# Encoder block: the Fourier channel transform multiplied into the weights, the softmax division moved to a^T

## The chip, the core and the metric

The kernel runs on one core of a Trainium2 chip. TensorE (PE) multiplies matrices into PSUM banks of 512 fp32 columns; its weight loads (PEld) run beside its matmuls. VectorE (DVE), ScalarE (ACT) and GpSimd (POOL) work element by element, and SyncE (SP) mostly issues DMAs. Each engine runs its own instructions strictly in order and waits on semaphores of the others. The metric is the device time of one execution in microseconds (us), the median of several runs. Beside it there is one profiled execution, with a trace of every instruction.

## What is computed

One encoder layer on two sequences, a sample of 1024 tokens and a prompt of 256, each with 16 learned meta tokens ahead (lengths 1040 and 272), D = 1024, in fp32:

```python
h = rms_norm(x, norm_mix_g)
z = h @ w_in                      # q 512 | k 128 | v 128 | f 512 | g_attn 1024 | g_four 1024
q = axial_rope(head_rms_norm(q, q_norm_g)); k = axial_rope(head_rms_norm(k, k_norm_g))
a = bidirectional_gqa(q, k, v) @ w_attn_o          # softmax(q k^T / 8) v, 8 heads, 2 kv heads
fo = real(fftn(f.reshape(l, 4, 128), axes=(positions, channels), norm="ortho")) @ w_four_o
x = x + (sigmoid(g_attn) * a + sigmoid(g_four) * fo) @ w_out
h2 = rms_norm(x, norm_ffn_g); u = h2 @ w_ffn_in
x = x + (silu(u[:, :2816]) * u[:, 2816:]) @ w_ffn_out
y = rms_norm(x, final_norm_g)     # without the meta tokens
```

## The kernel before

Each fp32 operand is split into a rounded part (hi) and its remainder (lo), both of type fp32r, and each product is three matmuls (`three`, L225 to L227: hi x hi, hi x lo, lo x hi). ACT makes the hi parts and DVE or POOL the lo parts (`split`, L205). The tokens stand in three chunks of columns: chunk 0 and 1 are the sample's 512 and 512, chunk 2 the prompt's 256 and, in the first stages, the 16 meta tokens.

The stages and where they lie in the span of the profile:

- `stage_a` (0 to 84 us): x is normed and transposed to hT, 256 columns at a time, and `fgemm` multiplies each new piece by the four blocks of w_f (tiles f), giving f^T for the four channel groups.
- `fourier`, q and k/v (to about 314). `fourier` folds f^T into even and odd parts along the positions (L501, L504, DVE), multiplies by the 128 x 128 channel transform in plain fp32 (`chan`: tiles ues, uos, uep, uop, L538 and L539), splits the results, and multiplies by position tables (fse, fso, fs for the sample, fpe, fpo for the prompt). An even half of 1040 positions has 521 rows, of 272 has 137, so the last piece of each has 9 rows. The results go to DRAM (f_d). The gates (16 units of 128 columns of w_g, by three chunks; tiles g, wg) are made by a generator, `gate_gen`; `weave` puts gate matmuls between those of the main stream by shares of their cost, chunk 0 here.
- The attention (to 664). For each block of 128 queries and each head: S (L892, six matmuls in the sample, one three-bank buffer), its negated row maximum on DVE (L897), the exponential with row sums on ACT (L904), the reciprocal and the division of p on DVE (L908, L909); then p is transposed in two to three "turns" a head (pt, L826, cast on ACT L828, remainder on DVE L829) and multiplied by v (pv, L846, L847); the result a goes to DRAM transposed (a_d). The gates of chunks 1 and 2 are the filler (`Filler`): a table FILL gives the cost of gate matmuls that are put in after each half of a head. What is left of them follows behind the last pv.
- The merge (675 to 771), written by hand in the order of issue: for each of eight row blocks i, `fourier(i)` (tiles fo) and the attention projection m for chunks 0, 2, 1, times the sigmoids of the gates (POOL L1091, L1139, DVE L1138, late casts L1145, L1146). `need(i)` makes the split weights of a block: two sums on DVE (L1034, L1035), casts on ACT (L1038), remainders on DVE (L1039). `load_af` loads a^T in five blocks of 1024 columns (two for chunk 0, one for chunk 2, two for chunk 1) and splits them on ACT (L209) and DVE (L210).
- `w_out` (to about 896, tiles wo, weights woh and wol), then the two feed-forward products, which the change doesn't touch.

Outside the hand-ordered pieces (the first block of `stage_a`, attention and merge) a scheduler sets the order of each engine from the program order and the dependencies. Working buffers are slots of 1056 columns, handed out again in the order in which they were put back, so a step can also wait for the last reader of a slot.

Of the kernel before, what the change touches and what calls it, by code (L numbers as in the profile page):

```python
# [47 lines left out]
QSTART = 22  # L48
KVSTART = 60
PARTS = 96  # L50
# [9 lines left out]
NL = NLS + NLP  # L60
HL = NL // 2
# [117 lines left out]
class Kernel:  # L179
# [19 lines left out]


# [106 lines left out]
    def stage_a(self, ps):  # L307
# [19 lines left out]
        def load_w():  # L327
            if len(wf) < 4:
                wf.append(self.load_split(a["w_f"][len(wf)], D, "wf", nc.vector))
# [3 lines left out]
        self.fT = [sl.get(f"fT{g}") for g in range(4)]  # L333
        self.fTp = [sl.get(f"fTp{g}") for g in range(2)]
# [24 lines left out]
        def fgemm(c, lo, hi):  # L359
            n = hi - lo  # L360
            for g in range(4):
                wh, wl = wf[g]
                pf = ps.tile([P, 512], F32, tag="mm", name=f"f{c}_{g}")
# [7 lines left out]
                if c < 2:  # L371
                    b = N_META + 512 * c + lo
                    nc.scalar.copy(self.fT[g][:, b : b + n], pf[:, :n])
                else:
                    b = (g % 2) * 272
                    fp = self.fTp[g // 2]
                    nc.scalar.copy(fp[:, b + N_META : b + 272], pf[:, :256])
                    nc.vector.tensor_copy(fp[:, b : b + N_META], pf[:, 256:272])
                    nc.vector.tensor_copy(self.fT[g][:, :N_META], pf[:, 256:272])
# [3 lines left out]
        nc.sync.dma_start(raw[:, :D], a["w_f"][0])  # L383
# [31 lines left out]
        fgemm(0, 0, 256)  # L415
# [3 lines left out]
        fgemm(0, 256, 512)  # L419
        tiles(3)  # L420
        load(4)
        fgemm(2, 0, 272)
        tiles(4)
        fgemm(1, 0, 512)
        for h, l in wf:
            sl.put(h, l)
# [63 lines left out]


    def fourier(self, ps):
        nc, a, sl = self.nc, self.a, self.sl

        E = [sl.get(f"fe{j}") for j in range(2)]
        O = [sl.get(f"fo{j}") for j in range(2)]
        Ep, Op = sl.get("fep"), sl.get("fop")

        def fold(src, b, L, e, eb, o, ob, eng):
            h = L // 2  # L500
            eng.tensor_tensor(  # L501
                e[:, eb + 1 : eb + h], src[:, b + 1 : b + h], src[:, b + L - 1 : b + h : -1], op=ALU.add
            )
            eng.tensor_tensor(  # L504
                o[:, ob + 1 : ob + h], src[:, b + 1 : b + h], src[:, b + L - 1 : b + h : -1], op=ALU.subtract
            )
            for p in (0, h):
                nc.vector.tensor_copy(e[:, eb + p : eb + p + 1], src[:, b + p : b + p + 1])
                nc.vector.memset(o[:, ob + p : ob + p + 1], 0.0)

        for g in range(4):
            b = (g % 2) * 521
            fold(self.fT[g], 0, LS, E[g // 2], b, O[g // 2], b, nc.vector)
            fold(self.fTp[g // 2], (g % 2) * 272, LP, Ep, g * 137, Op, g * 137, nc.vector)
            yield 1
        sl.put(*self.fT, *self.fTp)

        T = self.const.tile([P, 129], F32, name="T")
        nc.sync.dma_start(T[:], a["chan"])


        def chan(seq):
            n_tot = 521 if seq == "s" else 137
            nt = -(-n_tot // P)
# [1326 lines left out]
```

## Time and profile before

| | |
|---|---|
| median of 3 runs | 1728.25 us (1727.11 to 1728.6) |
| profiled execution, its own time | 1727.39 us |
| its span (first to last instruction) | 1725.6 us |
| granted TensorE clock, mean | 0.996 |
| DMA traffic | 197.80 MB, mean 115 GB/s |

The span is what the trace shows; all positions below are microseconds from its start. A row of the timeline has start, duration, engine, line, operation, output<-inputs and the shape; "[0.96 <-ACT fT L373]" behind it means that the engine stood idle for 0.96 us ahead of this row and that ACT's write of fT at line 373 ended last of what it waited for. Matmuls are pipelined: the durations of PE's rows overlap, and the distance of two starts is what one costs. A group row has the busy time and mean duration of many like instructions, and the idle time ahead of them.

### The profile page before, as it was taken

How to read it: one execution, taken by the hardware profiler on the slowest of the kernel's cores; microseconds unless marked ns; L12 is line 12 of the kernel's file. 1: busy time of each engine (PE TensorE's matmuls, PEld its weight loads, DVE VectorE, ACT ScalarE, POOL GpSimd, SP SyncE). 2: the span in 40 equal slices, each digit the busy share in tenths (PEclk: the TensorE clock that was granted, in tenths of full speed). 3: DMA queues.
4: the chain of work that ended last, by engine and by line, in shares of the span. 5: the costliest groups of instructions: out<-in, count | busy, mean ns of one | idle time of the engine just before them, and what ended most of it. 6: DMA issues, size and time to landing. Idle time of an engine off the chain costs nothing.

```text
span 1725.6 us, 25871 instructions
## 1 busy us (share of the span) xinstructions
PE 1679.1 (97%) x9837; PEld 1495.5 (87%) x9837; DVE 1116.3 (65%) x2089; ACT 719.4 (42%) x1429; POOL 278.7 (16%) x321
## 2 busy tenths in 40 slices
PE   7999999999999999989989999999999999999997
PEld 6888879878888888878879999999999998888886
DVE  5423544568888885652479676667666768765685
ACT  6322333456666665451355222222222234444444
POOL 3001333210130212663353000000000000000002
PEclk9999999999999999999999999999999999999999
DMA  5144331312112235534442222322232237653534
GB/s 191 57 140 145 116 116 51 124 53 71 50 57 63 65 116 195 177 110 135 160 158 82 84 71 91 103 91 83 95 103 80 76 123 259 204 179 99 161 99 153
DMA packets 90509, 197.80 MB, mean 115 GB/s; under 512 B 9773, under 2 KB 40137, under 8 KB 90384
## 3 DMA queue, kind: packets, MB, share of 16 engines
q1 hardware_dynamic: 81168, 178.97, 31.5%
q10 hardware_dynamic: 7824, 12.53, 2.1%
q0 software_dynamic: 1392, 4.63, 0.9%
q8 instruction: 77, 1.26, 0.3%
q14 instruction: 48, 0.39, 0.1%
HBM read 140.68 MB, written 55.42 MB: 114 GB/s over the span
## 4 chain that ended last, share of the span: by engine, by line
PE 83%; DVE 7%; issue 3%; ACT 3%; POOL 3%; DMA 2%; SPq 0%; POOLq 0%; ACTq 0%; DVEq 0%
PE i L225 10%; PE i L226 10%; PE i L227 10%; PE o L227 5%; PE o L226 5%; PE o L225 5%; PE g L225 4%; PE S L892 4%; PE g L227 4%; PE g L226 4%; PE pt L826 3%; PE pv L846 2%; PE pv L847 2%; PE wo L226 2%; PE wo L227 2%
## 5 line engine op out<-in xcount | busy, mean ns | idle before, releaser
L1345 ACT CAST w<-wi 128x512 fp32r<-128x512 f32 x168 | 103.9, 621 | 272.0 <-PE i L227 221.1
L225 PE MATMUL i<-A,w 128*128 128x384 f32 x616 | 208.9, 339 | 3.0 <-ACT w L1345 2.7
L227 PE MATMUL i<-A,w 128*128 128x384 f32 x616 | 208.0, 338 | 2.3 <-POOL w L1347 2.3
L226 PE MATMUL i<-A,w 128*128 128x384 f32 x616 | 208.2, 338 | 0.0
L227 PE MATMUL i<-Ah,w 128*128 128x256 f32 x616 | 173.0, 281 | 0.0
L226 PE MATMUL i<-Al,w 128*128 128x256 f32 x616 | 173.0, 281 | 0.0
L225 PE MATMUL i<-Ah,w 128*128 128x256 f32 x616 | 172.7, 280 | 0.0
L828 ACT CAST pT<-pt 128x512 fp32r<-128x512 f32 x156 | 90.7, 582 | 96.4 <-PE pt L826 91.4
L829 DVE TENSOR_TENSOR pT<-pt,pT 128x512 fp32r<-128x512 f32 x156 | 106.9, 686 | 27.1 <-ACT pT L828 25.0
L1347 DVE TENSOR_TENSOR w<-wi,w 128x512 fp32r<-128x512 f32 x154 | 105.2, 685 | 29.0 <-ACT w L1345 28.6
L234 POOL TENSOR_SCALAR fin0r<-fin0ss 128x1 f32<-128x1 f32 x1 | 0.8, 788 | 754.0 <-ACT X L242 754.0
L225 PEld LDWEIGHTS i<-A,w 128*128 128x128 f32 x616 | 116.5, 189 | 3.6 <-ACT w L1345 2.9
L897 DVE TENSOR_REDUCE sm<-S 128x1 f32<-128x1040 f32 (+1 forms) x80 | 86.5, 1081 | 51.1 <-PE S L892 46.8
L227 PEld LDWEIGHTS i<-A,w 128*128 128x128 f32 x616 | 116.2, 189 | 3.2 <-POOL w L1347 3.2
L226 PEld LDWEIGHTS i<-A,w 128*128 128x128 f32 x616 | 116.5, 189 | 0.0
L225 PEld LDWEIGHTS i<-Ah,w 128*128 128x128 f32 x616 | 116.0, 188 | 0.4 <-ACT w L1345 0.4
L227 PEld LDWEIGHTS i<-Ah,w 128*128 128x128 f32 x616 | 116.1, 189 | 0.0
L226 PEld LDWEIGHTS i<-Al,w 128*128 128x128 f32 x616 | 116.0, 188 | 0.0
L904 ACT ACTIVATE p<-S,sm 128x1040 f32<-128x1040 f32 (+1 forms) x80 | 80.2, 1002 | 33.6 <-DVE sm L897 29.2
L826 PE MATMUL pt<-ident,p 128*128 128x128 f32 (+1 forms) x624 | 93.4, 272 | 0.0
L227 PE MATMUL o<-wfo,act 128*128 128x512 f32 (+1 forms) x212 | 82.0, 387 | 2.3 <-DVE act L1479 2.3
L826 PEld LDWEIGHTS pt<-ident,p 128*128 128x128 f32 (+1 forms) x624 | 72.4, 134 | 10.7 <-DVE pT L829 0.2
(762 smaller groups left out, 4444.9 us busy)
## 6 DMA issues: line engine op xcount, KB each, us to landing
wi<-w_fi SPq DMA_DIRECT2D x48, 512.0 KB, 3.4
wg<-w_g SPq DMA_DIRECT2D x32, 512.0 KB, 3.7
act_d<-sc SPq DMA_DIRECT2D x77, 192.0 KB, 1.9
act<-act_d SPq DMA_DIRECT2D x37, 320.0 KB, 3.3
wfo<-w_fo SPq DMA_DIRECT2D x21, 512.0 KB, 5.2
X<-act_d SPq DMA_DIRECT2D x31, 320.0 KB, 3.0
act_d<-sc SPq DMA_DIRECT2D x77, 128.0 KB, 1.7
gate<-gs ACTq DMA_DIRECT2D x32, 256.0 KB, 2.0
```

The lines of the kernel that those rows point to most:

```text
L225: mm(out, sh, mh, start=first and i == 0, stop=False)
L226: mm(out, sh, ml, start=False, stop=False)
L227: mm(out, slo, mh, start=False, stop=last and i == n - 1)
L826: nc.tensor.transpose(pt[:rows, h * P : (h + 1) * P], me.ps4[h][:, col : col + rows], self.ident[:])
L828: nc.scalar.copy(pT[:rows, :512], pt[:rows, :])
L829: nc.vector.tensor_tensor(pT[:rows, 512:1024], pt[:rows, :], f32(pT[:rows, :512]), op=ALU.subtract)
L846: nc.tensor.matmul(me.pv[:], vst, pT[:rows, :512], start=j == 0, stop=False)
L892: nc.tensor.matmul(S[:, base + lo : base + hi], hq, self.kT[seq][g][v][:, lo:hi], start=v == 0, stop=v == 1)
L897: nc.vector.tensor_reduce(nb, S[:, base : base + L], axis=AX.X, op=ALU.max, negate=True)
L904: self.last_exp = nc.scalar.activation(p, S[:, base : base + L], AF.Exp, bias=nb, accum_out=total)
L1345: nc.scalar.copy(w[:, :512], src)
L1347: eng.tensor_tensor(w[:, 512:1024], src, f32(w[:, :512]), op=ALU.subtract)
```

## The change

Four parts.

1. *Fourier.* The channel transform is multiplied into w_f on the core (`channels`: 32 plain fp32 products of 128 x 128, tiles wc, split into wch and wcl). In place of f, h itself is folded: `folds` adds hi and lo back together on POOL (hs, and ep for the prompt), makes even and odd sums on DVE, and splits them (tiles eo) on ACT and DVE, for each of the eight blocks k of 128 rows of h. `fourier_in` multiplies the folded h by the combined weights, 36 matmuls for each k, into six banks u0 to u5, from which the same ue and uo are made as before. The prompt's 137 rows are reversed, padded and joined to the sample's 521, so that no 9-row pieces are left but zero-padded ones of 128. w_f itself is passed transposed. In `stage_a` the place of `fgemm` is taken by `first`, which makes the first four gate units; `gate_gen` makes the other twelve, with smaller FILL costs and other shares for `weave`.
2. *Softmax.* The row sums of four heads are kept (total), their reciprocals taken at once, turned into rows by a transpose on TensorE (into columns of S that are not used), copied by DVE and stored (rc_d). `load_af` loads them back, one row for 64 partitions, and multiplies a^T by them on DVE ahead of the split.
3. *Merge.* `need(i + 2)` stands ahead of the m products of i, where it stood behind the first of them.
4. *w_out.* Its first weights are split earlier (behind chunk 0 of the last block, where it was behind chunk 2), the remainder on DVE in place of POOL.

In the rows below, names are tiles with a running number. DVE in the middle of the attention, before; pt and pT are the turns, p the exponentials, sm the row maximum and reciprocal:

```order
L829 TENSOR_TENSOR pT_4453<-pt_4448,pT_4453 128x512
L897 TENSOR_REDUCE sm<-S_4465 128x1
L829 TENSOR_TENSOR pT_4479<-pt_4474,pT_4479 128x512
L908 RECIPROCAL sm<-sm 128x1
L909 TENSOR_SCALAR p_4439<-p_4439,sm 128x1040
L829 TENSOR_TENSOR pT_4496<-pt_4491,pT_4496 128x512
L897 TENSOR_REDUCE sm<-S_4505 128x1
```

The same place in the changed kernel, where total holds the sums of four heads:

```order
L991 RECIPROCAL total_4784<-total_4784 128x4
L896 TENSOR_TENSOR pT_5040<-pt_5035,pT_5040 128x512
L965 TENSOR_REDUCE sm<-S_5050 128x1
L896 TENSOR_TENSOR pT_5064<-pt_5059,pT_5064 128x512
L996 COPY rcT_5070<-S_5050 4x128
L896 TENSOR_TENSOR hT0l_260<-pt_5079,hT0l_260 128x512
L965 TENSOR_REDUCE sm<-S_5091 128x1
```

The division of 1040 columns is gone from every head; a reciprocal and a copy of 4 x 128 come in once in four.

DVE at the end of the attention, before; af are the loaded a^T blocks, afl their remainders, fst the fourier products of the first block:

```order
L1039 TENSOR_TENSOR wm_6875<-wma_6653,wm_6875 128x512
L210 TENSOR_TENSOR afl_6893<-af_6664,afh_6892 128x1024
L210 TENSOR_TENSOR afl_6920<-af_6666,afh_6919 128x1024
L210 TENSOR_TENSOR afl_6963<-af_6938,afh_6962 128x1024
L1039 TENSOR_TENSOR pT_6101<-wmf_6878,pT_6101 128x512
L1039 TENSOR_TENSOR wm_6983<-wma_6881,wm_6983 128x512
L1081 TENSOR_TENSOR fst_7004<-fst_7004,fo_6997 128x328
```

And in the changed kernel, where L1080 is the multiplication by the reciprocals' rows (rc):

```order
L1123 TENSOR_TENSOR hT0l_260<-wmf_6746,hT0l_260 128x512
L1123 TENSOR_TENSOR pT_6233<-wma_6749,pT_6233 128x512
L1080 TENSOR_TENSOR af_6760<-af_6760,rc_6761 128x1024
L1165 TENSOR_TENSOR fst_7037<-fst_7037,fo_7030 128x328
L1166 TENSOR_TENSOR fst_7037<-fst_7037,fo_7030 128x328
L216 TENSOR_TENSOR afl_6982<-af_6760,afh_6981 128x1024
L1080 TENSOR_TENSOR af_6975<-af_6975,rc_6976 128x1024
L1165 TENSOR_TENSOR fst_7058<-fst_7058,fo_7051 128x192
```

Before, three of the five blocks were split ahead of the first fourier rows (fst); now the multiplications and splits stand between and behind them.

DVE in the middle of the merge, before (wmf are the weights of the next fourier product, gt the gated sums):

```order
L1082 TENSOR_TENSOR fst_7347<-fst_7347,fo_7340 128x136
L1034 TENSOR_TENSOR wmf_7256<-wmf_7256 128x256
L1035 TENSOR_TENSOR wmf_7256<-wmf_7256 128x256
L1039 TENSOR_TENSOR wm_7125<-wmf_7256,wm_7125 128x512
L1039 TENSOR_TENSOR wm_7378<-wma_7259,wm_7378 128x512
L1138 TENSOR_TENSOR gt_7041<-m_7361,gt_7041 128x512
```

And in the changed kernel:

```order
L1166 TENSOR_TENSOR fst_7387<-fst_7387,fo_7380 128x136
L1118 TENSOR_TENSOR wmf_7296<-wmf_7296 128x256
L1119 TENSOR_TENSOR wmf_7296<-wmf_7296 128x256
L1123 TENSOR_TENSOR wm_7163<-wmf_7296,wm_7163 128x512
L1123 TENSOR_TENSOR wm_7014<-wma_7299,wm_7014 128x512
L1225 TENSOR_TENSOR gt_7074<-m_7408,gt_7074 128x512
```

On DVE nothing moved; on ACT the two casts of the weights now come ahead of the three sigmoids of the same block.

The diff, cut to its core:

```diff
-                wf.append(self.load_split(a["w_f"][len(wf)], D, "wf", nc.vector))
+                wf.append(self.load_split(a["w_g"][len(wf)], D, "wf", nc.vector))
...
-        fgemm(2, 0, 272)
+        first(2, 0, 256)
         tiles(4)
-        fgemm(1, 0, 512)
+        self.channels(ps, wt)
+        self.fold = self.folds()
+        next(self.fold)
+        first(1, 0, 512, self.fold)
...
+    def channels(self, ps, wt):
+        for k in range(KD):
+            for g in range(4):
+                nc.tensor.matmul(pt[:, c], wt[g][:, k * P : (k + 1) * P], self.T[:], start=True, stop=True)
+            for src, b, w in ((p4[:, :, :65], 0, 65), (p4[:, :, 65:], 260, 63)):
+                nc.scalar.copy(h, src)
+                nc.vector.tensor_tensor(l, src, f32(h), op=ALU.subtract)
+    def folds(self):
+        for k in range(KD):
+            for c, x, lo in ((0, s, N_META), (1, s, N_META + 512), (2, p, N_META)):
+                pool(x[:, lo : lo + CH_N[c]], h, l, op=ALU.add)
+            for z, op in ((e, ALU.add), (o, ALU.subtract)):
+                vec(z[:, :NS], s[:, :NS], s[:, LS : NS - 2 : -1], op=op)
+                vec(z[:, 544:FN], ep[:, 8 + NP_ - 1 : 7 : -1], p[:, NP_ - 1 :], op=op)
+                nc.scalar.copy(h[:, :FN], z)
+                vec(l[:, :FN], z, f32(h[:, :FN]), op=ALU.subtract)
+    def fourier_in(self, ps, tab):
+            for j, (b, m) in enumerate(cols):
+                for odd, (h, l) in enumerate(parts):
+                    nc.tensor.matmul(out, hm, w[0][:, s], start=False, stop=False)
+                    nc.tensor.matmul(out, hm, w[1][:, s], start=False, stop=False)
+                    nc.tensor.matmul(out, lm, w[0][:, s], start=False, stop=odd == 1 and k == KD - 1)
...
-    FILL = {"s": 610, "p": 400, "end": 640, "drain": 900}
+    FILL = {"s": 420, "p": 500, "end": 480, "drain": 900}
...
-        order = list(range(16))
+        order = list(range(N_FIRST, 16))
...
-                def scale(p=p, rc=rc, total=total):
-                    nc.vector.reciprocal(rc, total)
-                    nc.vector.tensor_scalar(p, p, rc, None, op0=ALU.mult)
+            def divide(bank, t=t, g=g, total=total, first=[]):
+                    first.append(nc.vector.reciprocal(total[:], total[:]))
+                nc.tensor.transpose(bank, total[:], self.ident[:])
+                nc.vector.tensor_copy(rc[:], bank)
+                    nc.sync.dma_start(dst, rc[x::2, :])
...
+                    nc.sync.dma_start(d[x * HD : (x + 1) * HD, :1024], src.partition_broadcast(HD))
...
+            nc.vector.tensor_tensor(r[:, :1024], r[:, :1024], d[:, :1024], op=ALU.mult)
...
             yield from fourier(i + 1)
+            if i:
+                need(i + 2)
...
-                    need(i + 2)
+                    if i == 0:
+                        need(2)
...
-                if c == 2 and i == 7:
+                if c == 0 and i == 7:
                     next(then)
...
-        units[0] = self.split(raw, 1024, "wo", nc.gpsimd, "s")
+        units[0] = self.split(raw, 1024, "wo", nc.vector, "s")
...
-            weave(ahead(q_pass, KVSTART, kv_pass), gates, 0.62)
-            weave(kv_pass, gates, 0.6)
+            weave(ahead(q_pass, KVSTART, kv_pass), gates, 0.28)
+            weave(kv_pass, gates, 0.62)
```

More of the change, by code (lines that the diff above doesn't have):

```diff
@@ L370, in fgemm @@
                 )
[L371 to L379, printed above, removed]
+                st = self.small.tile([P, 512], F32, tag="stage", name=f"fg{u}_{c}")
+                nc.scalar.copy(st[:, :n], pf[:, :n])
+                nc.scalar.dma_start(self.gates[u][c][:, lo:hi], st[:, :n])
+                if then is not None:
+                    sl.put(wh, wl)
+                    if u % 2 == 0:
+                        next(then)
         load(0)
         raw = sl.get("wf")
-        nc.sync.dma_start(raw[:, :D], a["w_f"][0])
+        nc.sync.dma_start(raw[:, :D], a["w_g"][0])
         rows = sl.get("gain")
@@ new lines, in fourier_in @@
+    def fourier_in(self, ps, tab):
+        nc, sl = self.nc, self.sl
+        cols = [(j * P, P) for j in range(4)] + [(512, 41), (553, P)]
+        banks = [ps.tile([P, 512], F32, tag="mm" if j < 4 else "tr", name=f"u{j}") for j in range(6)]
+        for k in range(KD):
+            while k not in self.eo:
+                next(self.fold)
+            parts = self.eo.pop(k)
+            w = [x[:, k % 2 * 512 : k % 2 * 512 + 512] for x in self.wc[k // 2]]
+            for j, (b, m) in enumerate(cols):
+                for odd, (h, l) in enumerate(parts):
+                    s = slice(260, 512) if odd else slice(260)
+                    out, hm, lm = banks[j][:m, s], h[:, b : b + m], l[:, b : b + m]
+                    if k or odd:
+                        nc.tensor.matmul(out, hm, w[0][:, s], start=False, stop=False)
+                    else:
+                        nc.tensor.matmul(banks[j][:m, :], hm, self.wz[:], start=True, stop=False)
+                    nc.tensor.matmul(out, hm, w[1][:, s], start=False, stop=False)
+                    nc.tensor.matmul(out, lm, w[0][:, s], start=False, stop=odd == 1 and k == KD - 1)
+                yield 0
+            for x in parts:
+                sl.put(*x)
+            if k + 2 < KD:
+                next(self.fold)
+            elif k + 2 == KD:
+                next(self.fold, None)
+            for _ in range((0, 0, 2, 0, 2, 0, 4, 2)[k]):
+                tab()
+            if k % 2:
+                sl.put(*self.wc[k // 2])
+        ue = [sl.get("ue", F32R) for _ in range(3)]
+        uo = [sl.get("uo", F32R) for _ in range(3)]
+        for x in uo[:2]:
+            nc.gpsimd.memset(f32(x.v(4, 256))[:, :, 252:256], 0.0)
+        nc.gpsimd.memset(f32(ue[2][:, :520]), 0.0)
+        nc.gpsimd.memset(f32(uo[2][:, :1024]), 0.0)
+        for j, (_, m) in enumerate(cols):
+            ev = banks[j][:m, :260].rearrange("p (g c) -> p g c", g=4)
+            b = j % 2 * 520
+            u = ue[j // 2]
+            for base, w, src in ((0, 64, ev[:, :, :64]), (256, 1, ev[:, :, 64:65])):
+                hv = u.v(4, w, b + base)[:m]
+                lv = u.v(4, w, b + 260 + base)[:m]
+                nc.scalar.copy(hv, src)
+                nc.vector.tensor_tensor(lv, src, f32(hv), op=ALU.subtract)
+            b = j % 2 * 512
+            u = uo[j // 2]
+            src = banks[j][:m, 260:512]
+            nc.scalar.copy(u[:m, b : b + 252], src)
+            nc.vector.tensor_tensor(u[:m, b + 256 : b + 508], src, f32(u[:m, b : b + 252]), op=ALU.subtract)
+        self.U = ue, uo
+        yield 8000
@@ L562, in u_e @@
+        yield from self.fourier_in(ps, tab)
+        us = self.U
         def u_e(uu, j, m, p, part):
@@ L1813, in layout @@
         "qk_g": np.concatenate([gq, gq[swap], gk, gk[swap]]),
-        "w_f": units(w[:, 768:1280]),
+        "w_ft": w[:, 768:1280].T.reshape(4, P, D),
         "w_g": units(w[:, 1280:]),
```

214 lines of the change are left out of this document (107 added, 107 removed).

## The prediction

> **What bounds the kernel now.** I read the busy times first, then the chain that ended last, then the busy times by stage.
>
> ```profile
> PE 1679.1 (97%) x9837; PEld 1495.5 (87%) x9837; DVE 1116.3 (65%) x2089; ACT 719.4 (42%) x1429; POOL 278.7 (16%) x321
> ...
> PE 83%; DVE 7%; issue 3%; ACT 3%; POOL 3%; DMA 2%; SPq 0%; POOLq 0%; ACTq 0%; DVEq 0%
> ```
>
> TensorE is busy for 97% of the span and makes 83% of the chain, so a matmul that goes away is worth its full pitch (start to start), unless a stall takes its place. The stages (from:to, length, then PE busy, weight loads, DVE, ACT, POOL) say where other engines matter:
>
> ```profile
> 0.00:84.00 84.00, 71.65 (x473) 65.25 (x473) 42.27 (x125) 41.75 (x95) 15.85 (x31) 1.00 0.38 128
> ...
> 340.00:664.00 324.00, 319.11 (x1911) 267.28 (x1910) 250.91 (x382) 198.95 (x366) 52.13 (x44) 1.00 0.24 74
> 664.00:675.00 11.00, 11.00 (x72) 9.92 (x72) 5.69 (x8) 6.55 (x11) 0.00 (x0) 1.00 0.98 322
> 675.00:771.00 96.00, 89.74 (x498) 78.22 (x496) 59.58 (x120) 49.59 (x102) 59.94 (x78) 1.00 0.42 135
> ```
>
> The attention (340 to 664) is nearly full; the merge (675 to 771) lacks 6 us of PE. From 664 to 675 PE runs 72 gate matmuls without a hole, after the last pv: filler that covers the first loads of the merge.
>
> **TensorE's work, by pitches.** Timeline rows of PE (start, duration, line, product<-inputs):
>
> ```profile
> 49.28 0.29 PE L225 MATMUL f<-hT2h,wfh 128*128 128x272 f32 x1
> 49.41 0.29 PE L226 MATMUL f<-hT2l,wfh 128*128 128x272 f32 x1
> ...
> 84.67 0.40 PE L226 MATMUL g<-hT0h,wgh 128*128 128x512 f32 x1
> 84.91 0.39 PE L227 MATMUL g<-hT0h,wgl 128*128 128x512 f32 x1
> 85.14 0.33 PE L538 MATMUL ues<-T,fe 128*128 128x65 f32 x2
> 85.30 0.39 PE L539 MATMUL uos<-T,fo 128*128 128x64 f32 x2
> 85.53 0.39 PE L538 MATMUL ues<-T,fe 128*128 128x65 f32 x2
> ...
> 113.34 0.29 PE L226 MATMUL fse<-tabc,ue 128*128 128x260 f32 x1
> 113.47 0.28 PE L227 MATMUL fse<-tabc,ue 128*128 128x260 f32 x1
> 113.68 0.38 PE L225 MATMUL fse<-tabc,hT0l 9*128 9x260 f32 x1
> 113.91 0.27 PE L226 MATMUL fse<-tabc,hT0l 9*128 9x260 f32 x1
> 114.02 0.28 PE L227 MATMUL fse<-tabc,hT0l 9*128 9x260 f32 x1
> 114.23 0.50 PE L225 MATMUL g<-hT0h,wgh 128*128 128x512 f32 x1
> ```
>
> Starts lie 0.23 us apart at 512 columns, 0.125 at 272, 0.12 at 260; an fp32 product of 64 or 65 columns is two records and takes 0.22.
>
> Removed. The first stage now multiplies h by four gate blocks where it multiplied by w_f, so its own count stays (96 matmuls of 272 columns become 256 columns), and the gate units lose 192 of 512 columns (192 x 0.231 = 44.4 us) and, with that swap, 96 of 272 (96 x 0.125 = 12.0). The channel products ues, uos, uep, uop go: 40 full ones of 0.22 and 16 of nine columns at half of that, 10.6 us. The nine-row pieces become full: from 113.47 to 114.23 is 0.76 where four even pitches are 0.48, 0.28 each for eight to ten pieces, 2.4 us. Sum 69.4.
>
> Added. u: eight k steps of 36 matmuls of 252 or 260 columns (6 of the 288 have 512): 282 x 0.119 + 6 x 0.23 = 34.9, or 4.35 us a k. wc: 32 fp32 products of 128 columns, which before doesn't have. From below they cost half of the 64-column product (0.11), from above twice it (0.44): 3.5 to 14 us. Its weights, 128 columns as well, weigh more than its columns (nine-column weights halve it), so I take 0.23, 7.4. The reciprocals' 20 small transposes at 0.11 to 0.2: 3. Sum 45.3.
>
> Net **-24.1 us** of PE work, with 17.6 to 28 as its ends, mostly wc's. By the counted rows, about 24 of the gate time leaves the attention heads and 10.5 leaves the filler of 664 to 675; a good 20 leaves q and kv, less what came in ahead of them.
>
> **Attention.** One head of the 1040-column kind (PE's S, DVE's maximum, ACT's exponential, DVE's division of the head before, PE's next S), PE's wait for the exponential over the whole run, and the S group of the short prompt heads (its last number is idle time):
>
> ```profile
> 497.18 1.12 PE L892 MATMUL S<-kT,qT 128*128 128x264 f32 x6
> ...
> 498.33 1.24 DVE L897 TENSOR_REDUCE sm<-S 128x1 f32<-128x1040 f32 x1 [0.44 <-PE S L892]
> ...
> 499.69 1.13 ACT L904 ACTIVATE p<-S,sm 128x1040 f32<-128x1040 f32 x1 [0.34 <-PE g L226]
> ...
> 500.27 0.76 DVE L909 TENSOR_SCALAR p<-p,sm 128x1040 f32<-128x1040 f32 x1
> ...
> 501.31 1.11 PE L892 MATMUL S<-kT,qT 128*128 128x264 f32 x6
> ...
> PE S L892 <- ACT p L904: 3.3, 5, 1.2
> ...
> L892 PE MATMUL S<-kTp,qT 128*128 128x272 f32 x32 | 7.2, 307 | 1.5 <-ACT p L904 1.3 <-ACT gs L457 0.2
> ```
>
> S has one buffer, so the next S follows the exponential: 497.18 to 500.82, and a hand-over, 3.7 us at least. This head took 4.13, filled by PE with two turns of pt and pv and six gate matmuls. The 64 heads hold 278 us of PE work before and 254 after, 4.35 and 3.97 each; heads of three turns stay far above 3.7, but those of two turns come to 3.6 to 3.8, where chain and work are even. The division (0.76) and its reciprocal leave DVE, which runs beside the chain and isn't late today (the maximum starts 0.03 after S), so that earns nothing by itself. What is late next is the exponential. Some 45 two-turn heads at under 0.1 us each: **+3.3 us** (0 to +10). The new transpose writes into unused columns of S, and DVE must copy it out before the next S; that is 0.2 us beside the exponential, in one head of four. The short prompt heads, whose S waits 1.5 us now, get more filler (500 for 400): **-1**.
>
> **The start of the merge.** Timeline of PE, of DVE and of ACT:
>
> ```profile
> 678.73 0.31 PE L227 MATMUL fo<-pT,pT 128*128 128x328 f32 x1
> 681.23 0.42 PE L1061 MATMUL fo<-pT 68*128 68x328 f32 x1 [2.19 <-ACT fst L1074]
> ...
> 667.84 1.23 DVE L210 TENSOR_TENSOR afl<-af,afh 128x1024 fp32r<-128x1024 f32 x1 [0.18 <-ACT afh L209]
> ...
> 679.93 0.94 ACT L1047 ACTIVATE gt<-gt 128x512 f32<-128x512 f32 x2 [2.29 <-DMA gate<-gs]
> ```
>
> Before, one stall of 2.35 us here. Now six gate matmuls (0.7 us) are all that is left behind the last pv. DVE must add ao, make the first fourier weights (to about 2.7 us after the pv), and then for each of five a^T blocks wait for a row load, multiply (no such row; it lies between the 0.76 of L909 and twice the split of the same size, 1.23; I take the split's) and split, interleaved with the fst rows (the second pair of order blocks). Following that order, a second-block row for chunk 2 is there at 15.4 and the last of chunk 1 at about 24.7, while PE is at m of chunk 1 at 17.2: it waits 2.3 at the start and about 6 there. 8.4 against 2.4 before: **+6 us** (+3 to +11). The ten row loads are queued on SP ahead of the next gates' loads, which have an iteration to spare.
>
> **The merge loop and w_out.** The third pair of order blocks shows that the weights' rows stand at the same place of DVE's order as before: only ACT's casts move ahead of its sigmoids. ACT waited for DVE there, not DVE for ACT, so I cost this move at **0** (-5 if the stalls at every fo went). For w_out:
>
> ```profile
> 770.43 1.11 DVE L1146 TENSOR_TENSOR ml<-gt,mh 128x512 fp32r<-128x512 f32 x1 [1.24 <-ACT mh L1145]
> ...
> 771.56 1.04 ACT L209 CAST woh<-wo 128x1024 fp32r<-128x1024 f32 x1
> ...
> 773.03 2.34 POOL L210 TENSOR_TENSOR wol<-wo,woh 128x1024 fp32r<-128x1024 f32 x1
> ...
> 772.65 0.50 PE L225 MATMUL wo<-woh,mh 128*128 128x512 f32 x1 [1.83 <-ACT woh L209]
> 775.42 0.50 PE L226 MATMUL wo<-wol,mh 128*128 128x512 f32 x1 [2.27 <-POOL wol L210]
> ```
>
> The cast moves ahead of one more cast (to about 770.4), the remainder to DVE behind the row of 770.43 (771.5 to 772.7, 1.23). PE then resumes for good at 772.8 instead of 775.42: **-2.7** (-1 to -4.5). Behind it on DVE wait the rows of m in chunks 2 and 1, which w_out needs only with its last k.
>
> **Folds.** A k costs DVE two rows of 521 (0.70 by 73.10 below), two of 137 (0.30) and two remainders of 681 (0.89 by the ratio of columns), 3.8 us; POOL two sums of 512 (1.29) and one of 256, 3.2; PE 4.35. k 0 and 1 are made beside wc and the four first-stage products (30 us); later ones wait for slots that u frees three halves later. Each alone is shorter than PE's step, so I count **+0.5** for late folds. The waits at both ends (ahead of f1 for wc's casts, behind u for six banks to be evacuated, 1 us each) stand against the channel products' own evacuation, which had PE swap between their banks and gates: **0**.
>
> ```profile
> 73.10 0.70 DVE L501 TENSOR_TENSOR fe<-fT 128x519 f32<-128x519 f32 x1 [4.01 <-ACT fT L373]
> ...
> L690 POOL TENSOR_TENSOR ropeA<-ropeA 128x512 f32<-128x512 f32 x10 | 12.9, 1286 | 0.0
> ...
> 777.12 2.37 POOL L210 TENSOR_TENSOR wol<-wo,woh 128x1024 fp32r<-128x1024 f32 x1 [1.75 <-ACT woh L209]
> ...
> 777.54 2.23 DVE L1146 TENSOR_TENSOR ml<-gt,mh 128x256 fp32r<-128x256 f32 x1
> ...
> 757.94 0.42 DVE L1146 TENSOR_TENSOR ml<-gt,mh 128x256 fp32r<-128x256 f32 x1
> ```
>
> The last three rows speak against this: a DVE row of 256 columns, 0.42 at 757.94, took 2.23 at 777.54 and ended 0.28 after POOL's. The Trainium skill, SBUF — State Buffer, section "Who interferes with whom", has the rule: a DVE instruction with two SBUF inputs contends with a GpSimd instruction that reads SBUF, and the shared port is an exclusive lock. The trace agrees in these rows.
>
> **Sum.** -24.1 + 3.3 - 1 + 6 + 0 - 2.7 + 0.5 + 0 = -18.0. From the profiled execution's 1727.39 (median of the runs shown 1728.25, so no correction worth making) that is **1709.4**, 1.0% faster.
>
> **Rivals.** *Folds one after the other*: all rows of DVE and POOL of a k exclude each other, 3.8 + 3.2 = 7 us a k against 4.35. The five or six k that u overtakes cost up to 2.65 each, less what was made ahead: +7 to +15, 1716 to 1724. For it, the rows above; against it, three slots of lead and the start-up part of each row, which does overlap. Chance 0.15. *Attention's chain is longer than 3.7*, since maximum and exponential stand in order behind splits and casts of the turns: 0.15 us a head is +10, 1719. For it, this head's 0.12 between maximum and exponential; against it, S has waited for the exponential five times in 80 heads. Chance 0.15. *Covered better*: the rows' loads and multiplications are early, the merge loop's stalls go and wc costs 3.5: 1698 to 1703. Chance 0.15. *Slower than before*: the head's chain rises to where the removed gates save nothing. Its place is the copy out of S and the in-order exponential; with 64 heads the 18 us are gone once every head takes 0.28 more than the 4.02 forecast (3.97 and its share of the 3.3), that is 4.30, and at 4.5 the time is 1740. This head's chain is 3.7 with all its hand-overs. Chance 0.05. *The change doesn't do what it says*, u or the gate count being other: the order shows both as counted; below 0.02, inside the others.
>
> **How the numbers follow.** Forecast 0.50, with its own 1703 to 1715; rivals as given. I take 1699 to 1722, which leaves out the ends of the first and third rival and the slower case, about 0.2. Measurement can tell about 0.2%, 3.5 us: faster 0.90, same 0.05 (upper ends of folds and attention), slower 0.05.
>
> **What would show it.** PE busy down by 24 us; heads with periods at 3.7 to 3.8; a PE hole of 2 us before the first fo and 6 before m of chunk 1; wo starting 1 us behind the last m; u without holes above 0.3 us. Wrong if u shows a hole at every k, if heads stay at 4.1 with less work in them, or if the merge's holes exceed 11 us.

## The result, and the profile after

| | median (runs) | ratio to before, 95% interval |
|---|---|---|
| before | 1728.39 us (4) | |
| changed | 1743.29 us (1742.25 to 1743.73, 4) | 1.0087 (1.0069 to 1.0104) |

The changed kernel is 0.9% slower; 1709.4 was forecast, and 1743 lies outside the range of 1699 to 1722. The profiled execution took 1742.25 us, its span 1740.5.

The page of the changed kernel, busy times and then the chain that ended last:

```profile
PE 1667.6 (96%) x9809; PEld 1479.5 (85%) x9809; DVE 1093.8 (63%) x1973; ACT 724.4 (42%) x1462; POOL 302.8 (17%) x348
...
PE 60%; DVE 9%; ACT 4%; issue 4%; POOL 2%; DMA 2%; SPq 0%; POOLq 0%; ACTq 0%; DVEq 0%
```

PE is busy for less time in a longer span, and its share of the chain fell from 83% to 60%: in more places PE waits for another engine. Where that costs time needs a table by stage. For each kind of matmul (product, columns, weight shape, and for pv the line) I took the median pitch times the count as the stage's *work*; the rest of its length is *stall*:

| stage | length before, after | work before, after | stall before, after |
|---|---|---|---|
| to the first S (x, q, k/v, Fourier) | 314.4, 324.1 | 295.6, 300.4 | 18.7, 23.5 |
| 16 short heads | 40.8, 44.3 | 37.2, 40.8 | 3.6, 3.5 |
| 64 long heads, to the last pv | 308.1, 311.4 | 306.0, 280.5 | **2.1, 31.0** |
| last pv to the first fo | 11.7, 1.1 | 11.6, 1.0 | 0.1, 0.1 |
| merge (first fo to w_out) | 97.7, 107.9 | 86.7, 87.1 | **11.0, 20.8** |
| w_out | 120.9, 118.2 | 116.6, 116.6 | 4.4, 1.6 |
| the two feed-forward products | 832.1, 833.4 | 810.8, 811.9 | 21.2, 21.5 |

The work fell by 26 us and the stalls rose by 41. Nearly all of the rise is in two stages. Their windows (from:to, length, then busy time and count of PE, weight loads, DVE, ACT, POOL; granted clock; DMA share and GB/s), before the change (long heads, first fo, m):

```profile
355.20:663.30 308.10, 304.24 (x1824) 255.21 (x1822) 242.96 (x360) 191.67 (x347) 49.56 (x42) 1.00 0.24 72
675.00:685.30 10.30, 8.11 (x55) 7.84 (x54) 4.95 (x11) 6.61 (x14) 3.51 (x7) 1.00 0.57 209
685.30:772.60 87.30, 81.63 (x445) 70.37 (x443) 56.11 (x111) 44.55 (x91) 57.00 (x73) 1.00 0.41 127
```

and the same stages of the changed kernel:

```profile
368.40:679.90 311.50, 289.01 (x1699) 230.50 (x1697) 192.78 (x266) 189.02 (x339) 38.37 (x34) 1.00 0.21 65
680.00:692.70 12.70, 10.89 (x61) 10.21 (x60) 10.36 (x15) 6.42 (x11) 4.68 (x6) 0.87 0.98 268
692.70:788.90 96.20, 86.61 (x446) 73.12 (x445) 60.63 (x116) 46.33 (x94) 57.77 (x73) 0.95 0.47 143
```

In the long heads there are 125 matmuls fewer in a stage 3 us longer; DVE lost 50 us of work there, and it earned nothing. In the merge the clock, 1.00 before, is below 1.

**The long heads.** Each unit of four heads has one head with three turns (its second) and three with two. Means over the 16 units: the exponential's start behind the end of the maximum, the next S behind the end of the exponential, and the period from S to S. The other pieces hardly change: S takes 1.11 to 1.20, the maximum starts 0.04 behind it and takes 1.24, the exponential takes 1.13.

| head | exponential late, before / after | next S, before / after | period before / after |
|---|---|---|---|
| first | 0.07 / 0.07 | 0.54 / 0.28 | 4.16 / 3.93 |
| second | 1.29 / 1.29 | 0.89 / 0.74 | 5.72 / 5.60 |
| third | **0.05 / 0.83** | 0.46 / 0.21 | 4.04 / **4.57** |
| fourth | 0.05 / 0.07 | 0.42 / 0.24 | 4.01 / 3.92 |

One third head of the changed kernel, from the timeline of all engines:

```profile
522.53 1.24 DVE L965 TENSOR_REDUCE sm<-S 128x1 f32<-128x1040 f32 x1 [0.74 <-PE S L960]
...
523.69 0.68 DVE L896 TENSOR_TENSOR pT<-pt,pT 128x512 fp32r<-128x512 f32 x1
523.83 0.27 PE L994 MATMUL S<-ident,total 128*4 128x128 f32 x1 [0.43 <-DVE sm L965]
...
524.29 0.27 DVE L996 COPY rcT<-S 4x128 f32<-4x128 f32 x1
...
524.65 1.13 ACT L973 ACTIVATE p<-S,sm 128x1040 f32<-128x1040 f32 x1 [1.09 <-DVE rcT L996]
...
525.92 0.39 PE L960 MATMUL S<-hT0l,qT 128*128 128x264 f32 x1 [0.21 <-ACT p L973]
```

Read it from the bottom: the next S waits for the exponential, the exponential for DVE's copy of four rows, the copy for the remainder of a turn that stands ahead of it on DVE, and PE's transpose for the maximum, since all of them touch the tile S. The maximum had ended at 523.77. The exponential could have gone at 523.8 and went at 524.65. The waits of PE in the long heads, before:

```profile
PE S L892 <- ACT p L904: 2.0, 2, 1.2
PE pv L846 <- DVE ao L854: 0.4, 1, 0.4
```

and after (total us, times, longest):

```profile
PE S L994 <- DVE sm L965: 6.9, 16, 0.4
PE S L960 <- ACT p L973: 6.4, 13, 1.9
PE pv L913 <- DVE ao L921: 6.1, 10, 0.8
```

Three waits: the transpose's in all 16 third heads; S for the exponential; and one more that the forecast has no word of, pv for ao. It stands in the second heads, where the first pv of a unit follows the last pv of the one before it into the same bank, which ACT and DVE must have read first. Gate matmuls between the two give PE something to do. Before, every such place had some, about 0.8 us or more in all but one, as in these rows, where no wait over 0.15 us is left:

```profile
504.02 0.39 PE L847 MATMUL pv<-pT,v 16*128 16x512 f32 x1
504.34 0.50 PE L225 MATMUL g<-hT1h,wgh 128*128 128x512 f32 x1
...
505.13 0.60 PE L826 MATMUL pt<-ident,p 128*128 128x128 f32 x4
505.86 0.50 PE L846 MATMUL pv<-pT,v 128*128 128x512 f32 x1
```

After, five places have none and PE waits 0.8 us there, five have 0.46 us of them and it waits 0.4. One of the five without:

```profile
520.12 0.50 PE L913 MATMUL pv<-pT,v 128*128 128x512 f32 x1 [0.80 <-DVE ao L921]
```

**The merge.** PE's rows of the timeline at which the changed kernel waits, and the windows around them:

```profile
682.95 0.42 PE L231 MATMUL fo<-pT,hT0l 128*128 128x328 f32 x1 [1.65 <-ACT hT0l L1122]
...
696.72 0.38 PE L232 MATMUL m<-afl,pT 128*128 128x256 f32 x1 [0.88 <-DVE afl L216]
...
701.74 0.77 PE L231 MATMUL m<-wm,pT 128*128 128x512 f32 x1 [3.44 <-ACT wm L215]
703.09 0.79 PE L232 MATMUL m<-hT0l,pT 128*128 128x512 f32 x1 [0.58 <-DVE hT0l L216]
...
704.11 0.63 PE L231 MATMUL m<-wm,pT 128*128 128x512 f32 x1
704.54 0.63 PE L232 MATMUL m<-hT0l,pT 128*128 128x512 f32 x1
```

```profile
684.00:688.00 4.00, 4.00 (x19) 4.00 (x18) 3.30 (x5) 1.56 (x3) 1.40 (x2) 0.59 1.05 268
702.00:712.00 10.00, 8.27 (x20) 5.79 (x20) 6.38 (x9) 3.54 (x6) 2.42 (x2) 0.50 0.72 222
```

PE waits for the split of a^T blocks, and behind the hole of 3.44 us its clock is granted at half: the last two rows of m lie 0.43 apart where 512 columns take 0.23 elsewhere. The blocks come slowly because each is multiplied, cast on ACT and split on DVE in turn, with the fst rows between them; the last multiplication also waits for its load (rc). DVE's rows there:

```profile
692.83 1.49 DVE L1080 TENSOR_TENSOR af<-af,rc 128x1024 f32<-128x1024 f32 x1
695.44 1.23 DVE L216 TENSOR_TENSOR afl<-af,afh 128x1024 fp32r<-128x1024 f32 x1 [1.12 <-ACT afh L215]
...
699.35 1.26 DVE L1080 TENSOR_TENSOR af<-af,rc 128x1024 f32<-128x1024 f32 x1
701.72 1.32 DVE L216 TENSOR_TENSOR hT0l<-af,wm 128x1024 fp32r<-128x1024 f32 x1 [1.11 <-ACT wm L215]
703.87 1.23 DVE L1080 TENSOR_TENSOR af<-af,rc 128x1024 f32<-128x1024 f32 x1 [0.84 <-DMA rc<-rc_d]
```

From a multiplication to the end of its split is 3.7 to 3.8 us, of which DVE stands idle for 1.1.

### The profile page after: what moved, and what is told of

Same layout as the page of the kernel before. It is cut to its first block, busy times and chain, and to the rows that moved or that the text cites. A ratio compares the mean times of both kernels' runs of the same rounds, so it can differ in the third digit from the quotient of the medians.

```text
span 1740.5 us, 25983 instructions
## 1 busy us (share of the span) xinstructions
PE 1667.6 (96%) x9809; PEld 1479.5 (85%) x9809; DVE 1093.8 (63%) x1973; ACT 724.4 (42%) x1462; POOL 302.8 (17%) x348
## 2 busy tenths in 40 slices
DMA packets 91581, 198.62 MB, mean 114 GB/s; under 512 B 10006, under 2 KB 41474, under 8 KB 91456
## 4 chain that ended last, share of the span: by engine, by line
PE 60%; DVE 9%; ACT 4%; issue 4%; POOL 2%; DMA 2%; SPq 0%; POOLq 0%; ACTq 0%; DVEq 0%
PE i L231 9%; PE i L233 9%; PE i L232 9%; PE o L233 5%; PE o L232 5%; PE o L231 5%; PE S L960 4%; DVE sm L965 2%; PE pt L893 2%; ACT p L973 2%; PE pv L913 1%; PE wo L232 1%; PE wo L233 1%; PE wo L231 1%; PE g L231 1%
## 5 line engine op out<-in xcount | busy, mean ns | idle before, releaser
L896 DVE TENSOR_TENSOR pT<-pt,pT 128x512 fp32r<-128x512 f32 (+1 forms) x138 | 94.5, 686 | 78.5 <-ACT pT L895 77.3
L895 ACT CAST pT<-pt 128x512 fp32r<-128x512 f32 (+1 forms) x138 | 80.1, 581 | 82.6 <-PE pt L893 79.2
L233 PE MATMUL o<-wfo,act 128*128 128x512 f32 (+1 forms) x212 | 82.1, 388 | 2.1 <-DVE act L1566 2.1
L232 PE MATMUL o<-wfo,act 128*128 128x512 f32 (+1 forms) x212 | 82.0, 387 | 0.0
```

The source lines that it names most:

```text
L232: mm(out, sh, ml, start=False, stop=False)
L233: mm(out, slo, mh, start=False, stop=last and i == n - 1)
L895: nc.scalar.copy(pT[:rows, :512], pt[:rows, :])
L896: nc.vector.tensor_tensor(pT[:rows, 512:1024], pt[:rows, :], f32(pT[:rows, :512]), op=ALU.subtract)
```

## The experiments

Times are medians; ratios are to the kernel before on the same chip, whose medians were 1726.7 to 1728.4 us. So up to 1.7 us between two times can be the chip's.

**The two large parts, apart.** e2 is the changed kernel with the softmax part undone: reciprocal and division of p on DVE in each head as before, no total, rc or transposes, a^T loaded and split as before; it keeps the changes of the merge and of w_out. e3 is the kernel before with the softmax part alone.

```diff
 e2:
-                if divide and h:
-                    divide(S[:4, 0:P] if t < 8 else S[:4, base + 384 : base + 512])
-                    divide = None if h == 2 else divide
+                if scale:
+                    scale()
...
+                def scale(p=p, rc=rc, total=total):
+                    nc.vector.reciprocal(rc, total)
+                    nc.vector.tensor_scalar(p, p, rc, None, op0=ALU.mult)
...
-            nc.vector.tensor_tensor(r[:, :1024], r[:, :1024], d[:, :1024], op=ALU.mult)
```

> The changed kernel with its softmax part undone: the division stands on p again, in every head, and a^T is loaded and split as before. The Fourier part, the filler costs, the merge and w_out stay changed. Theory A: the third head of each group falls to 3.8 to 3.9, PE's holes before and in the first merge block (20.8 us over pitch from the first fo to the first wo, 11.0 before) fall by the five multiplications, some 6 us, and the time is 1715 to 1726, faster than before. Rival B: the heads' mean stays at 4.4 to 4.5; only the merge gains, 1735 to 1738. Rival C (DVE's division was hidden only by the full filler, and now lengthens the chain): heads of 4.2 and more, about 1740.

> The kernel before with the softmax part alone. Theory A: the third head goes from 4.15 to about 4.5, 16 times 0.35, and the copy of gates behind the last pv hides most of the loads: slower than before by 4 to 10 us, 1732 to 1738. Rival B: with the full filler the step in S costs nothing, and DVE has 0.9 us less in every head: 1724 to 1729.

e2: 1721.19 us, ratio 0.9963 (0.9948 to 0.9977), as theory A said. e3: 1756.05 us, 1.0163 (1.0148 to 1.0178), far above what any theory said. So the softmax part costs 22 us on top of the Fourier part and 28 alone, and the Fourier part, with those of the merge and w_out, gains 7, not the 26 by which PE's work falls. By stages, e2 against the changed kernel: stalls of the long heads 18.2 for 31.0, of the merge 10.8 for 20.8. The third heads' exponential is 0.05 late again, their period 3.81. In e3, with nothing taken from PE, it is 0.84 late and the period 4.76; stalls there rise from 2.1 to 14.0 and in the merge from 11.0 to 22.3. The two places are the same, with or without the Fourier part. In e3 the gate matmuls that follow the last pv take as long as before, 11 us, so it is not their loss that makes the start of the merge late. What the Fourier part's gain still loses in e2 is 16 us of stall in the long heads.

**The step ahead of the exponential.** Three tries to take it from the changed kernel. e1 gives the transpose a bank of its own (the turns' pt banks, in place of columns of S):

```diff
-                    divide(S[:4, 0:P] if t < 8 else S[:4, base + 384 : base + 512])
+                    divide(ps.tile([P, 512], F32, tag="tr", name="rcT")[:4, :P] if h == 2 else None)
```

> The changed kernel, with the transposed reciprocals written into one of the two banks of the turns (pt) instead of into unused columns of S. Theory A (the attention is held by the step in S: the transpose waits for the row maximum and the exponential waits for DVE's copy, once in four heads): PE's waits of 0.6 us at the transpose (16 times, 9.5 us) go, the third head of each group falls from 4.5 us to 3.8 to 3.9, and the time falls by 10 to 18 us, to 1725 to 1733. Rival B (the heads are simply short of filler, and their chains of 3.7 to 5.8 us stand whatever the step does): waits move from the transpose to the next S, the heads' mean stays at 4.5, and the time stays within 3 us of 1743.

1739.66 us, 1.0068 (1.005 to 1.0086): 3.6 less, between the two theories. The third heads' exponential is on time (0.05), but their period is still 4.30, and a new wait has come, as the waits of e1 in the long heads show:

```profile
PE pt L893 <- DVE pT L896: 5.4, 15, 0.9
```

The turns have two banks. Where the small transpose takes one, the next turn gets the bank of the turn just before it and waits for that one's remainder. The step had been moved, not removed, so this run could not decide. e5 stores the reciprocals by DMA straight from their 128 x 4 tile, without transpose or copy:

```diff
-                nc.tensor.transpose(bank, total[:], self.ident[:])
...
-                    nc.sync.dma_start(dst, rc[x::2, :])
+                for k in range(4):
+                    dst = self.rc_d[c][k % 2].rearrange("(k n o) -> k n o", k=4, o=1)[2 * g + k // 2, off : off + P]
+                    nc.sync.dma_start(dst, total[:, k : k + 1])
```

> The changed kernel, with each unit's reciprocals stored to rc_d straight from the 128x4 tile by four small DMAs, so that PE's transpose, DVE's copy and their place in front of the third head's exponential are gone (16 long and 4 short units). Theory A (the step through S holds the third head's exponential back: it starts 0.83 us after the maximum where it started 0.05, 16 heads): the third heads fall from 4.57 to 3.9 us, 16 x 0.67 = 10.7, and the end comes some 10 to 13 us sooner: 1730 to 1734. Rival B (the third heads are held by something else of this part, the lost division or its order on DVE): they stay above 4.3 and the time is within 4 us of 1743. Rival C: the 2,560-odd four-byte pieces a chunk are late for the merge's row loads, and the first fo or m waits for them: heads as in A, but the time within 4 us of 1743.

1799.35 us (1787.86 to 1816.64), 1.0393 (1.0325 to 1.0461), worse than every case that was written down: the stalls of the long heads went to 96.9 in the profiled execution (1810.49). It carries 80 such stores of 128 pieces of 4 bytes, and ACT's work waits on DMAs in the middle of the heads:

```profile
ACT p L973 <- DMA a_d<-ao: 25.0, 3, 11.3
...
ACT pT L895 <- DMA rc_d<-total: 17.7, 2, 9.8
```

So it tells nothing of the step. e9 keeps transpose and copy as they were and takes four units at a time, 16 rows instead of four:

```diff
-            total = self.small.tile([P, 4], F32, tag="total", name=f"total{t}{g}", bufs=3)
+            if t % 2 == 0 and g == 0:
+                total = self.small.tile([P, 16], F32, tag="total", name=f"total{t}", bufs=2)
...
+            if t % 2 == 0 or g == 0:
+                divide = None
```

> The changed kernel with one transpose and one copy for every four units (16 rows at a time) instead of one for each: four of the 16 third heads of the long units' stretch keep the step, no DMA of small pieces. Theory A (the step ahead of the third head's exponential): 12 or 13 heads fall from 4.57 to 3.9, 12 x 0.67 = 8, time 1734 to 1737. Rival B (something else of this part holds those heads): heads without the step stay above 4.3, time within 3 us of 1743.

1733.85 us, 1.0038 (1.0026 to 1.0051): 9.4 less, 7.7 as differences to the kernel before, close to the 8 of theory A. Of the 16 third heads of the stage the four with the step have the exponential 0.82 to 0.88 late and take 4.47 to 4.55; the twelve without it have it 0.03 to 0.09 late and take 3.70 to 4.24. The waits of the two kinds, in e9:

```profile
PE S L995 <- DVE sm L966: 1.7, 4, 0.4
...
ACT p L975 <- DVE rcT L997: 4.2, 4, 1.1
```

Four waits where the changed kernel has 16. So the step is the cause in these heads: with it the exponential comes 0.8 us later, and the head takes 0.65 us more (4.50 for 3.85). The long heads' stalls fall from 31.0 to 24.1.

**What the Fourier part loses in the heads.** e8, e10, e11 and e12 start from e2. e8 moves gate filler from the second heads (three turns) to the others:

```diff
+                more = 0 if t >= 8 else -300 if h == 1 else 100
```

> Fourier part without the softmax part (as the run before of that name, 1721.2 us) with filler moved between heads: 300 ns a half less in each long unit's second head (three turns, 5.60 us), 100 a half more in the three others (two turns). Theory F (a two-turn head cannot be shorter than S 1.17 + maximum 1.24 + exponential 1.13 and hand-overs 0.35 = 3.9 us, and its own work of 3.7 leaves PE idle for 0.2): two-turn heads stay at 3.9 or rise to 4.0, three-turn ones fall to about 5.0, so 16 x (5.6 - 5.0) less 48 x 0.05: 7 us sooner, 1712 to 1716, stalls of the long heads 18 to about 10. Rival G (filler is not what sets a head; PE waits at the turns' pv and transposes): two-turn heads rise by 0.2 to 4.1 and the time stays within 2 us of 1721.

1720.64 us, 0.9965 (0.9951 to 0.9979): no change, as rival G said. The second heads fell nearly as theory F said (5.60 to 5.17), the others rose as G said (from 3.81 to 3.95 up to 4.01 to 4.09), and the sum of four stayed at 17.3. The second heads kept their hole ahead of the first pv, now with no filler in it: 14 of them wait 0.8 us, where five do in e2. So moving filler had lengthened one wait while it shortened the heads, and this run alone does not tell what bounds a two-turn head. Rows of one hole in e8's timeline:

```profile
530.18 0.66 PE L893 MATMUL pt<-ident,p 128*128 128x128 f32 x4
531.63 0.50 PE L913 MATMUL pv<-pT,v 128*128 128x512 f32 x1 [0.80 <-DVE ao L921]
```

e11 therefore puts filler into that hole (1000 ns between the exponential and the third turn, none behind it), and e10 instead lays the nine turns of a unit so that the head with three has its two together behind the exponential:

```diff
 e11:
+                more = 0 if t >= 8 else 580 if h == 1 else -27
...
-                yield "end" if i + 1 == len(units) else seq, 0 if queue else 1000, True
+                yield "end" if i + 1 == len(units) else seq, (0 if t >= 8 else -420 if h == 1 else -27) if queue else 1000, True
 e10:
-                for _ in range(-(-me.left() // (2 * (ready + 4 - n) - k))):
+                for _ in range((me.left() if me.t < 8 else -(-me.left() // (2 * (ready + 4 - n) - k)) * (2 * (ready + 4 - n) - k)) // (2 * (ready + 4 - n) - k)):
```

> The same kernel without the softmax part, turns as they were, with filler of the long units moved: 1000 ns between the second head's exponential and its third turn (420 before), none behind that turn, 393 a half in the other heads. Theory H: the first pv's wait for ao (0.56 to 0.96 us in the second heads) is covered, second heads fall from 5.60 to about 5.1, two-turn ones stay at their chain of 3.9: 16 x 0.4, 6 us, 1713 to 1717. Rival I: second heads stay at 5.5 or more, within 3 us of 1721.

> Fourier part without the softmax part (1721.2 us), with the long units' nine turns laid the other way round: one a half, and the ninth as the last, behind the first head's exponential, where it stood ahead of the second head's. Theory H (the second head's 5.60 us come from two casts ahead of its exponential, 1.29 us late, and from the first pv of the unit following at once on the last one's evacuation by ACT and DVE): second heads fall from 5.60 to 4.0, first ones rise from 3.94 to 4.6 to 5.0, a unit from 17.3 to at most 16.9; stalls of the long heads 18 to 10 or less, 1708 to 1715. Rival I (units are bound by PE's own work at 4.38 a head and by two-turn heads at 3.9; the place of the ninth turn is without effect): within 3 us of 1721.

e11: 1713.58 us, 0.992 (0.9905 to 0.9935). e10: 1715.63 us, 0.9935 (0.9921 to 0.995). Both as theory H said, e10 at 0.6 us above its range and e11's second heads falling less than the 5.1 it gave. Second heads fall to 5.34 (e11) and 4.06 (e10, whose first heads, now with three turns, rise to 4.70), the wait of pv for ao goes from 6.0 us in e2 to none in e11 and to one of 0.2 in e10, and the long heads' stalls from 18.2 to 12.7 and 10.2. What is left stands, by its releaser, at S behind the exponential: heads with two turns are at 3.86 to 4.06, about the length of their chain. e12 starts from e10 and takes 265 ns a half of filler from the first heads, which now have three turns, for the three others:

> The kernel with the ninth turn last (1715.6 us) with filler moved as well: 265 ns a half less in the long units' first heads (three turns, 4.70 us), 88 more in the three others. Theory F+H (first heads are bound by PE's own work, the others by the chain of 3.9 with 0.1 to 0.2 of PE idle): first heads fall to about 4.3, the others stay within 0.05 of 3.9 to 4.05, 16 x (0.4 - 0.15) = 4 us, 1710 to 1713. Rival (the others are already bound by PE or by something else that filler does not hide): they rise by 0.15 each and the time stays within 2 us of 1715.6.

1715.13 us, 0.9927 (0.991 to 0.9944): the rival's time was right. First heads fall from 4.70 to 4.28, but the second rise from 4.06 to 4.54, far more than its 0.15. **e11 beats both kernels**: 0.8% under before, 1.7% under the change, and it is the change without its softmax part and with its filler moved.

**The merge.** e6 issues the a^T and reciprocal loads from POOL's queue; e7 leaves out the multiplications, and with them the softmax's division; e4 puts `need(i + 2)` back where it was.

```diff
 e6:
-                nc.sync.dma_start(r.v(per, n), src)
+                nc.gpsimd.dma_start(r.v(per, n), src)
 e7:
-            nc.vector.tensor_tensor(r[:, :1024], r[:, :1024], d[:, :1024], op=ALU.mult)
 e4:
-            if i:
-                need(i + 2)
...
+                    need(i + 2)
```

> The changed kernel, with the ten a^T row loads and the reciprocals' broadcast loads issued from POOL's queue instead of SP's. Theory D (the start of the merge is late because these loads stand on SP behind the gates' loads, which wait for slots: the last row load was issued after 6.39 us behind them): the stalls from the first fo to w_out fall from 20.8 to about 11 us and the time by 6 to 10, to 1733 to 1737. Rival E (DVE's multiplications and splits are the late thing, the loads had time): stalls stay at 18 to 21, time within 3 us of 1743.

> The changed kernel without the five multiplications of the a^T blocks (the softmax's division is left out; all loads stay). Theory D (loads on SP are late): the stalls from the first fo to w_out stay above 17 us, time within 3 us of 1743. Rival E (DVE's work is late): five rows of 1.1 to 1.75 us go, stalls fall by 5 to 8, and the time to 1735 to 1738.

> The changed kernel with need(i + 2) put back behind the first product of m. By the order, DVE's rows stand at the same place either way and only ACT's casts change sides with the sigmoids: the same as the changed kernel within 1 us (1742 to 1744). If the move hides stalls at each fo (0.9 us, five times), 1747.

e6: 1744.58 us, 1.0099 (1.0084 to 1.0114); stalls of the merge 22.0. Theory D's gain did not come, but the run does not clear the loads: POOL issued the last block's row load 14.0 us behind the first fo, SP 14.4, so the loads were hardly earlier, and in e6 DVE waits 2.24 and 1.30 us for reciprocals ahead of its second and third multiplication. e7: 1737.98 us, 1.0061 (1.0044 to 1.0077); stalls 14.8 for 20.8, as rival E said. The multiplications are 6 of the 10 us that the softmax part costs here. The other 4 were not taken apart. PE's hole at m of chunk 1 is shorter in e7, but it is there:

```profile
702.57 0.49 PE L231 MATMUL m<-wm,pT 128*128 128x512 f32 x1 [1.90 <-ACT wm L215]
```

ACT's cast ahead of it waited 5.59 us for the load of the last a^T block (af<-a_d), which was issued 11.0 us behind the first fo, where e2 issued its last one 4.3 behind. The changed `load_af` asks for one block ahead where it asked for two, and it adds ten loads of 256 KB for the reciprocals, while DMA is at full share, as e7's window shows (0.90 in e2's first 11.5 us):

```profile
683.40:694.90 11.50, 9.78 (x54) 9.04 (x53) 8.63 (x16) 7.31 (x14) 2.13 (x4) 0.85 1.03 277
```

Which of these makes the load late no run tells. e4: 1746.04 us, 1.0105 (1.009 to 1.012), 2.7 more than the change, with intervals that overlap; 1742 to 1744 was expected. Of the 2.7 only 0.7 is stall of the merge (21.5 for 20.8). Moving `need` did no harm, and its gain, if there is one, is below 3 us.

## Why the prediction was wrong

The sum was -18.0; the two profiled executions differ by +14.9. The 33 us between them are, by term:

- **PE's work**: -24.1 forecast, -26.1 measured. Right. wc came to 7.2 us of pitches (64 records at 0.112) for 7.4. The page's busy time fell by only 11.5, so it was the wrong meter: a 512-column row counts 0.40 but costs 0.23 when the next one follows, so each new hole adds to the busy time, and rows at half clock count more (0.63).
- **Attention, long heads**: +3.3 forecast (at most +10), +28.9 measured. **This is the step that failed**, and 25.6 of the 33. Two sentences of it were wrong. The first: "The new transpose writes into unused columns of S, and DVE must copy it out before the next S; that is 0.2 us beside the exponential". It is ahead of the exponential, not beside it. That the columns are unused does not help here; the waits follow the tile, so transpose, copy and exponential run in turn, and a turn's remainder gets in between on DVE. 0.78 us in 16 heads is 12.5; e2 has 12.8 less stall, and e9 6.9 less where twelve of the 16 lack the step, so it is worth 9 to 13. The order rows ahead of the prediction had the maximum, the remainder and the copy in this sequence, with maximum and copy on the same tile S. The second: two-turn heads "come to 3.6 to 3.8, where chain and work are even", at under 0.1 each. Their work was right (3.7 to 3.8), but the chain was put at 3.7 "at least" from one head and then used as its value. In the first heads it is 3.94: S 1.18, 0.04, the maximum 1.24, 0.07, the exponential 1.13, and 0.28 to the next S. And three-turn heads "stay far above 3.7" was read as safe, while their filler had been covering the evacuation of pv: the wait for ao, 0.4 us before, is 6.1 after, and e11 and e10 have 5.5 and 8 us less stall than e2. These two are the 16 us that e2 keeps; by the same pitches 6 of them stand in the second heads and 10 in the others. The rival "attention's chain is longer than 3.7", with its 10 us and 1719, came near in its price, as e2's 1721 shows, but not in its reason: in two-turn heads without the step the exponential is 0.05 to 0.07 late, after as before.
- **Short heads**: -1 forecast, -0.1 measured.
- **Start of the merge**: +6 (+3 to +11) forecast, +9.8 measured for the whole merge. In its range, and the holes are where they were forecast. The 1.8 at the first fo was forecast as 2.3; at m of chunk 1 the holes are 3.44, 0.58, 0.68 and 0.46, 5.2 for 6. Two things were missed. The clock: by the pitches of rows whose granted clock was below 0.75, half rate cost 3.9 us here, nothing before and 1.0 in e7, so half of what the multiplications cost is clock. And the loads: "queued on SP ahead of the next gates' loads" does not hold for the last block, whose load went out at 695.42, behind six gate loads that had held SP for 6.39 us. The lost filler, from which the forecast started, cost nothing: e2, without it, stalls 10.8 us in the merge, and e3, with it, 22.3.
- **`need`**: 0 forecast; e4 agrees within its interval.
- **w_out**: -2.7 forecast, -2.8 measured.
- **Late folds**: +0.5 forecast; u waits 1.9 us in all for DVE's eo, in three k. Folds one after the other would have cost 7 to 15; that rival fell.
- **The ends of u and the rest**: 0 forecast; the stages outside attention, merge and w_out gained some 5 us of stall, those 1.9 among them, in pieces below 2.3, which no run took apart.

The rival "slower than before" had named the place (the copy out of S and the in-order exponential), the point at which it decides (4.30 us a head) and the price at 4.5 (1740). Measured: 4.52 and 1743. It was given 0.05, because "this head's chain is 3.7 with all its hand-overs" was a chain of before, without the new step in it. The step alone would not have done it: 12.5 us of the 18 that were forecast leave a gain of 5. Together with the chain and the wait for ao, 16 us, it makes the change slower.

## What to carry to other kernels

When filler leaves a stage that was full, write out the chain of each kind of its iterations (here heads with two and with three turns), with the new instructions in their place of each in-order engine and with the tile, not the columns, as what they wait for; and look for waits that the filler had been hiding, such as the evacuation of a single bank. A small step that touches a single-buffered tile can cost its whole round trip over the engines (0.8 us here), not its own 0.27 us; do it once for many units. Division moved from 64 covered places to five uncovered ones is not a saving.

## What the runs showed of the hardware

- A hole can make the work behind it dearer. The granted clock was 0.50 from about 684.7 to 688 in the changed kernel, behind a hole of 1.65 us, and from 702 to 712 behind one of 3.44 with shorter ones following; before, with a hole of 2.19 at the first fo, it stayed at 1.00. The Trainium skill, TensorE: Matmul & The Clock Gate, section "The HAM clock gate", has the half rate and puts it behind an idle window of about 3.4 us, in windows that run freely. The half rate agrees (0.43 for 0.23), and the first stretch is about one such window long. That a hole of 1.65 us can be enough (in e2 as well: 0.50 from 671 to 674 behind a hole of the same length), and one of 2.19 not, is what these traces add.
- 80 stores of 128 four-byte pieces brought the packets from 91,581 to 102,942 (e5) and the time up by some 50 us (ratio 1.0393 for 1.0087), although they carry 40 KB.
